# A one-core decoder step: splitting gate and output weights in the query phase and keeping the parts off chip

## Chip, core and metric

The kernel runs on one core of a Trainium2 chip. The metric is the time of one execution in microseconds of device time; the median of several runs is compared. TensorE (PE) multiplies matrices, VectorE (DVE), ScalarE (ACT) and GpSimd (POOL) work on tiles in SBUF, SyncE (SP) issues transfers. ACT and POOL issue transfers too.

## The reference, cut to what matters

```python
def rmsnorm(x, g):
    y = x * rsqrt(mean(x * x, -1) + 1e-6); return y * g
# xp: 1024 prompt tokens, xs: 8 new tokens; w_in is 1024 x 2840, w_out 1024 x 1024
q, ckv, skv, wkv, gl, za, u, zp = split(rmsnorm(x, norm_g) @ w_in, ...)
kv_c = silu-MLP over overlapping 32-token blocks of ckv       # compressed keys and values
o_attn = sum over 3 branches of sigmoid(gl) * softmax-attention(q, branch's K, V)
o_pool = ((trailing mean of u over 2/4/8/16) - u) @ w_pool * pool_scale
mix = concat([o_attn * silu(za), o_pool * silu(zp)])
y = rmsnorm(x + mix @ w_out, final_g)
```

The same is done for the 8 new tokens against a paged cache of 256 positions ("decode"). Everything is float32.

## The kernel before

A float32 product is made of three faster ones: each operand is split into a high part (a copy to float32r) and a low part (the rest), and high x high, high x low and low x high are summed in PSUM. Splitting weights is a copy on ACT and a subtraction, mostly on DVE (`split_w`, L142; `load_tile`, L387).

The program goes through these phases, which overlap:

1. Keys and values of all tokens (L303 to L376).
2. The query phase. The compression of the compressed branch (L460 to L525) and the four query tiles (L528 to L542) stand next to each other and are mixed by a scheduler, which orders the instructions of each engine when the program is built, by the priority that follows from the program text and by when it reckons each one ready. A query tile is `load_tile` for 128 columns of w_in and three `feat_unit`s (L400) of 24 matmuls, for token chunks of 384, 384 and 264 columns. The results of a unit go to one of two PSUM banks in turn (`ps_any`, L71); ACT and DVE empty it, and the query parts go off chip to q_d through ACT's queue. The compression runs twice ("kind" 0 and 1: keys and values): for three groups, POOL's queue brings four `pr` tiles (L437 from the new keys, L440 gathered from the cache), PE transposes them (`z_ps`, L475), ACT and DVE split them into zh and zl, and PE multiplies them with cmp_w1 (`h_ps`, L489 to L491). H (L497) is the activation, then follow kc_ps (kind 0) or vc_ps and vcs_ps (kind 1), and POOL stores Kcs and Vcs to kc_d.
3. The pooling phase (L801 to L859): per group a tile u (three feat_units, copied by ACT at L808) and a tile sz (three more), and in between, with high priority, the decode (L548).
4. The attention (L1159 to L1196): 32 units of `stage1` (scores S, softmax) and `stage2` (transposes tp, products into O). Between their matmuls `paced_fill` puts filler work: `za_fill` (L970) with the gate path's weights, loaded by `load_tile` and multiplied like a feat_unit; then, per token tile, the output product with the output weights, which `load_wo` (L990) loads and splits into the space of the chunk of x that za_fill has finished with. `load_q` (L727) brings the query parts back four units ahead.

`cp` and `qp` are the pools of the query phase, on the left side of SBUF; `pu` and `pp` those of the pooling phase, on the right side. Tiles that lie on the same bytes wait for each other.

Of the kernel before, what the change touches and what calls it, by code (L numbers as in the profile page):

```python
# [7 lines left out]
F32 = mybir.dt.float32  # L8
# [28 lines left out]
def r32(ap):  # L37
    return ap.bitcast(F32)
# [3 lines left out]
def hybrid_step_kernel(ctx, tc, xp, xs, ccmp, cslc, cwin, spool, ptab, norm_g, w_in, cmp_pe, cmp_w1,  # L42
# [36 lines left out]
    b_d = dram.tile([4, 128, TOK], F32, name="b_d")  # L79
    g_d = dram.tile([NB, 24], F32, name="g_d")  # L80
    kc_d = dram.tile([2, 128, 128], F32, name="kc_d")


    ident = pers.tile([128, 128], F32, name="ident")
# [57 lines left out]
    def split_w(hi, lo, raw, eng=None):  # L142
        nc.scalar.activation(hi, raw, AF.Copy)
        (eng or nc.vector).tensor_sub(lo, raw, r32(hi))
# [252 lines left out]
    def w_cols(c0):  # L397
        return w_in.rearrange("(k p) c -> p k c", p=128)[:, :, c0:c0 + 128]
# [126 lines left out]
            nc.gpsimd.dma_start(kc_d[1], Vcs)  # L525


    for pt in range(4):  # L528
        hi, lo = load_tile(w_cols(C_Q + pt * 128))
        for c in range(3):  # L530
            p, t0, n = feat_unit(hi, lo, c)
            m = min(n, T - t0)
            qt_ = qp.tile([128, 2, 384], F32R, name="qhl")
            qh, ql = qt_[:, 0], qt_[:, 1]

            nc.scalar.activation(qh[:, :m], p[:, :m], AF.Copy, scale=-0.125)
            nc.vector.scalar_tensor_tensor(ql[:, :m], p[:, :m], -0.125, r32(qh[:, :m]),
                                           op0=OP.mult, op1=OP.subtract)
            if n > m:
                nc.vector.tensor_scalar(qs_t[:, pt, :], p[:, m:n], 0.125, None, op0=OP.mult)  # L540
            nc.scalar.dma_start(q_d[:, pt * 128:(pt + 1) * 128, t0:t0 + m].rearrange("f p t -> p f t"),
                                r32(qt_[:, :, :m]))  # L542
# [427 lines left out]
    def za_fill():  # L970
        w = {}
        for pt, c in ZORD:
            if pt not in w:
                w[pt] = load_tile(w_cols(C_ZA + pt * 128))
            hi, lo = w[pt]
            for t0, n in CHUNKS[c:c + 1]:
                p = ps_j()
                for k in range(8):
                    nc.tensor.matmul(p[:, :n], hi[:, k, :], xh[c][:, k, :], start=k == 0, stop=False)  # L979
                    nc.tensor.matmul(p[:, :n], hi[:, k, :], xl[c][:, k, :], start=False, stop=False)  # L980
                    nc.tensor.matmul(p[:, :n], lo[:, k, :], xh[c][:, k, :], start=False, stop=k == 7)  # L981
                    if k == 7:
                        gate(pt, t0, n, p)
                    yield
            if pt == 3:
                with tc.high_priority(2000):
                    load_wo(c)
        xt_es.close()

    def load_wo(c):  # L990

        rows = WROWS[c]
        w = xtp.tile([128, 2, CHUNKS[c][1] * 8], F32R, name=f"wo{c}", tag=f"x{c}")
        w = w[:, :, :512 * len(rows)].rearrange("p f (k c) -> p f k c", c=512)
        for j in range(0, len(rows), 2):
            half, k = rows[j]
            raw = rp.tile([128, 2, 512], F32, name="wo_raw", tag="r")
            nc.sync.dma_start(raw, w_out[k * 128:(k + 2) * 128, half * 512:half * 512 + 512]
                              .rearrange("(k p) c -> p k c", p=128))
            for kk in range(2):  # L1000
                nc.scalar.activation(w[:, 0, j + kk], raw[:, kk], AF.Copy)
                (nc.vector, nc.gpsimd)[kk].tensor_sub(w[:, 1, j + kk], raw[:, kk], r32(w[:, 0, j + kk]))
                O_[half, k + kk] = w[:, 0, j + kk], w[:, 1, j + kk]

    def open_out():
        fp, op = (ctx.enter_context(tc.tile_pool(name=n, bufs=1, side="right", reuse_waits="tile"))
# [275 lines left out]
```

## Time and profile before

| | us |
|---|---|
| median of 3 runs (lowest, highest) | 639.88 (638.89, 640.13) |
| the profiled execution's own time | 638.69 |
| its span, first to last instruction | 637.0 |
| PE busy | 622.3 |
| DVE busy | 423.4 |
| ACT busy | 367.3 |
| POOL busy | 270.7 |

The difference between time and span, 1.7 us, lies around the instructions. Busy time of PE says that a matmul was under way, not that the engine worked at its peak. The rows below name engine, line, operation, the tile written and the tiles read; an arrow and a name behind a wait tell what ended it.

### The profile page before, as it was taken

How to read it: one execution, taken by the hardware profiler on the slowest of the kernel's cores; microseconds unless marked ns; L12 is line 12 of the kernel's file. 1: busy time of each engine (PE TensorE's matmuls, PEld its weight loads, DVE VectorE, ACT ScalarE, POOL GpSimd, SP SyncE). 2: the span in 40 equal slices, each digit the busy share in tenths (PEclk: the TensorE clock that was granted, in tenths of full speed). 3: DMA queues.
4: the chain of work that ended last, by engine and by line, in shares of the span. 5: the costliest groups of instructions: out<-in, count | busy, mean ns of one | idle time of the engine just before them, and what ended most of it. 6: DMA issues, size and time to landing. Idle time of an engine off the chain costs nothing.

```text
span 637.0 us, 12211 instructions
## 1 busy us (share of the span) xinstructions
PE 622.3 (98%) x4160; PEld 578.5 (91%) x4160; DVE 423.4 (66%) x1253; ACT 367.3 (58%) x947; POOL 270.7 (43%) x412
## 2 busy tenths in 40 slices
PE   8999999999999999999999999999999999999995
PEld 5999999999999899999899899789999988898895
DVE  6754234637364647466887999778978787877653
ACT  5654233526223333217887988777877777776652
POOL 6144004314035615005556767645554556444510
PEclk9999999999999999999999999999999999999999
DMA  8436106956224433333313357313113030101101
GB/s 281 152 90 157 34 1 201 314 196 181 74 79 133 138 102 95 92 110 101 100 35 99 100 182 214 107 30 101 37 50 100 18 100 16 67 19 67 51 2 66
DMA packets 63742, 65.13 MB, mean 102 GB/s; under 512 B 4488, under 2 KB 55120, under 8 KB 63640
## 3 DMA queue, kind: packets, MB, share of 16 engines
q1 hardware_dynamic: 53631, 44.55, 23.4%
q0 software_dynamic: 4000, 12.76, 6.2%
q10 hardware_dynamic: 6048, 7.05, 3.2%
q8 instruction: 33, 0.54, 0.4%
q14 instruction: 30, 0.24, 0.1%
HBM read 50.98 MB, written 15.68 MB: 105 GB/s over the span
## 4 chain that ended last, share of the span: by engine, by line
PE 93%; DVE 2%; ACT 1%; issue 1%; DMA 1%; POOL 1%; DVEq 0%; POOLq 0%; ACTq 0%
PE pj L1053 14%; PE S L777 10%; PE tp L902 9%; PE pa L404 7%; PE pa L406 7%; PE pa L405 7%; PE O L920 5%; PE O L919 5%; PE pa L277 4%; PE pa L275 3%; PE pa L276 3%; PE pj L979 2%; PE pj L980 2%; PE pj L981 2%; PE xtp_ps L230 1%; PE pj L1057 1%
## 5 line engine op out<-in xcount | busy, mean ns | idle before, releaser
L908 DVE TENSOR_TENSOR pl<-tp,ph 128x512 fp32r<-128x512 f32 (+1 forms) x136 | 89.9, 670 | 22.7 <-ACT ph L907 22.0
L777 PE MATMUL S<-KT,qt 128*128 128x320 f32 (+10 forms) x400 | 98.2, 346 | 3.0 <-DVE sm L736 3.0
L907 ACT ACTIVATE ph<-tp 128x512 fp32r<-128x512 f32 (+1 forms) x136 | 78.0, 580 | 38.3 <-PE tp L902 28.7
L404 PE MATMUL pa<-x,ws_hi 128*128 128x384 f32 (+1 forms) x288 | 93.7, 325 | 0.0
L406 PE MATMUL pa<-x,ws_lo 128*128 128x384 f32 (+1 forms) x288 | 92.9, 323 | 0.0
L405 PE MATMUL pa<-x,ws_hi 128*128 128x384 f32 (+1 forms) x288 | 92.7, 322 | 0.0
L1053 PE MATMUL pj<-wo,mh 128*128 128x512 f32 (+1 forms) x272 | 84.1, 387 | 0.0
L920 PE MATMUL O<-pl,V 128*128 128x256 f32 x264 | 75.7, 305 | 0.2
L919 PE MATMUL O<-ph,V 128*128 128x256 f32 x264 | 74.0, 296 | 0.0
L777 PEld LDWEIGHTS S<-KT,qt 128*128 128x128 f32 x400 | 63.7, 189 | 9.0 <-DVE sm L736 3.0
L796 POOL TENSOR_SCALAR Ps<-Ps,sm,gates 128x64 f32<-128x64 f32 (+5 forms) x88 | 62.9, 722 | 19.9 <-DVE sm L792 7.3
L789 ACT ACTIVATE Ps<-Ps,sm 128x64 f32<-128x64 f32 (+4 forms) x96 | 60.2, 628 | 16.4 <-DVE sm L736 14.8
L404 PEld LDWEIGHTS pa<-x,ws_hi 128*128 128x128 f32 x288 | 54.2, 188 | 0.5
L405 PEld LDWEIGHTS pa<-x,ws_hi 128*128 128x128 f32 x288 | 54.2, 188 | 0.4 <-issue 0.3
L406 PEld LDWEIGHTS pa<-x,ws_lo 128*128 128x128 f32 x288 | 54.2, 188 | 0.2
L277 PE MATMUL pa<-w_hi,x 128*128 128x256 f32 (+1 forms) x184 | 52.9, 288 | 1.2 <-DVE x L236 1.2
L275 PE MATMUL pa<-w_hi,x 128*128 128x256 f32 (+1 forms) x184 | 53.6, 292 | 0.0
L1053 PEld LDWEIGHTS pj<-wo,mh 128*128 128x128 f32 x272 | 47.2, 188 | 6.1 <-ACT mh L1205 0.3
L920 PEld LDWEIGHTS O<-pl,V 128*128 128x128 f32 x264 | 49.8, 189 | 3.1 <-DVE pl L908 0.6
L276 PE MATMUL pa<-w_lo,x 128*128 128x256 f32 (+1 forms) x184 | 52.4, 285 | 0.0
L1053 PE MATMUL pj<-wo,ml 128*128 128x512 f32 (+1 forms) x136 | 52.1, 383 | 0.0
L919 PEld LDWEIGHTS O<-ph,V 128*128 128x128 f32 x264 | 49.9, 189 | 1.8
(302 smaller groups left out, 1556.1 us busy)
## 6 DMA issues: line engine op xcount, KB each, us to landing
ws_raw<-in_w_in SPq DMA_DIRECT2D x32, 256.0 KB, 3.1
qt<-q_d SPq DMA_DIRECT2D x64, 128.0 KB, 2.9
x_t<-in_x_prompt SPq DMA_DIRECT2D x8, 512.0 KB
wo_raw<-in_w_out SPq DMA_DIRECT2D x8, 512.0 KB, 4.3
r<-in_x_prompt SPq DMA_DIRECT2D x8, 512.0 KB, 3.1
out<-r SPq DMA_DIRECT2D x7, 512.0 KB, 3.1
q_d<-qhl ACTq DMA_DIRECT2D x8, 384.0 KB, 4.0
out<-kvf ACTq DMA_DIRECT2D x5, 512.0 KB, 3.1
```

The source lines that it names most:

```text
L275: nc.tensor.matmul(p[:n, :cn], xh[c][:, k, ts_], hi[:, k, :cn], start=k == 0, stop=False)
L276: nc.tensor.matmul(p[:n, :cn], xh[c][:, k, ts_], lo[:, k, :cn], start=False, stop=False)
L277: nc.tensor.matmul(p[:n, :cn], xl[c][:, k, ts_], hi[:, k, :cn], start=False, stop=k == 7)
L404: nc.tensor.matmul(p[:, :n], hi[:, k, :], xh[c][:, k, :], start=k == 0, stop=False)
L405: nc.tensor.matmul(p[:, :n], hi[:, k, :], xl[c][:, k, :], start=False, stop=False)
L406: nc.tensor.matmul(p[:, :n], lo[:, k, :], xh[c][:, k, :], start=False, stop=k == 7)
L777: nc.tensor.matmul(S[:, :ln], qt[:, f, h, :], KT[:, kv, k0 + a:k0 + a + ln], start=f == 0, stop=f == 1)
L907: nc.scalar.activation(ph[:, :m], tp[:, :m], AF.Copy)
L908: nc.vector.tensor_sub(pl[:, :m], tp[:, :m], r32(ph[:, :m]))
L919: nc.tensor.matmul(O[:, :256], vv, ph[:, a * 256:(a + 1) * 256], start=False, stop=False)
L920: nc.tensor.matmul(O[:, :256], vv, pl[:, a * 256:(a + 1) * 256], start=False, stop=last)
L1053: nc.tensor.matmul(p, a[:, k % 4, :], w, start=first and kk == 0, stop=last and kk == 2)
```

## The change

While the query phase runs, 24 pieces are staged: 8 halves of the four za weight tiles and 16 pieces of w_out, six ahead of each query tile. A piece is loaded by POOL's queue into `sraw` (2 buffers), split by ACT and DVE into `sw` (high and low part side by side, 2 buffers) and stored by POOL's queue to zw_d or wo_d. Later `load_za` and `load_wo` fetch both parts through SP's queue, straight into the tiles that the matmuls read. Nothing is split in the attention any more.

```diff
+    wo_d = dram.tile([2, 8, 128, 2, 512], F32, name="wo_d")
+    zw_d = dram.tile([4, 2, 128, 2, 512], F32, name="zw_d")
...
+    to_stage = [(zw_d[pt, h], w_cols(C_ZA + pt * 128)[:, 4 * h:4 * h + 4], 4) for pt in range(4) for h in range(2)]
+    to_stage += [(wo_d[half, k], w_out[k * 128:(k + 1) * 128, half * 512:half * 512 + 512], 1)
+                 for rows in WROWS for half, k in rows]
+
+    def stage_some(n):
+        for dst, src, k in to_stage[:n]:
+            raw = cp.tile([128, 512], F32, name="sraw", bufs=2)
+            nc.gpsimd.dma_start(raw.rearrange("p (k c) -> p k c", k=k) if k > 1 else raw, src)
+            w = cp.tile([128, 2, 512], F32R, name="sw", bufs=2)
+            split_w(w[:, 0], w[:, 1], raw)
+            nc.gpsimd.dma_start(dst, r32(w))
+        del to_stage[:n]
+
+    def load_za(pt):
+        hi = ws.tile([128, 8, 128], F32R, name="ws_hi", bufs=2)
+        lo = ws.tile([128, 8, 128], F32R, name="ws_lo", bufs=2)
+        for h in range(2):
+            for f, w in enumerate((hi, lo)):
+                nc.sync.dma_start(r32(w[:, 4 * h:4 * h + 4].rearrange("p k c -> p (k c)")), zw_d[pt, h, :, f])
+        return hi, lo
+
     for pt in range(4):
+        stage_some(6)
         hi, lo = load_tile(w_cols(C_Q + pt * 128))
...
-                w[pt] = load_tile(w_cols(C_ZA + pt * 128))
+                w[pt] = load_za(pt)
...
-        for j in range(0, len(rows), 2):
-            half, k = rows[j]
-            raw = rp.tile([128, 2, 512], F32, name="wo_raw", tag="r")
-            nc.sync.dma_start(raw, w_out[k * 128:(k + 2) * 128, half * 512:half * 512 + 512]
-                              .rearrange("(k p) c -> p k c", p=128))
-            for kk in range(2):
-                nc.scalar.activation(w[:, 0, j + kk], raw[:, kk], AF.Copy)
-                (nc.vector, nc.gpsimd)[kk].tensor_sub(w[:, 1, j + kk], raw[:, kk], r32(w[:, 0, j + kk]))
-                O_[half, k + kk] = w[:, 0, j + kk], w[:, 1, j + kk]
+        for j, (half, k) in enumerate(rows):
+            nc.sync.dma_start(r32(w[:, :, j]), wo_d[half, k])
+            O_[half, k] = w[:, 0, j], w[:, 1, j]
```

The new tiles take 12 KB per partition of `cp`, so `qp` lies 12 KB higher. Addresses in the built programs, in bytes of a partition: before, cp and qp end at 126752 and the two u tiles of the pooling phase lie at 130304 to 134496 and 134496 to 138688. With the change sraw lies at 120608 to 124704, the second sw buffer at 128800 to 132896, and the two qhl buffers of the query parts at 132896 to 139040.

The scheduler orders all engines anew. In the new file, lines of the query phase and after have numbers that are up to 26 higher. Names behind "waits" are semaphores: PE, DVE and Activation count those engines' instructions, DMASW0 to DMASW7 count landings of POOL's transfers in turn, DMAHW those of SP's and ACT's.

ACT at the end of the compression, before: the first u copies (L808) stand ahead of H of kind 1 (L497).

```order
L541 DMA q_d<-qhl 128x2x256 [waits DVE_49]
L808 ACTIVATE u<-pa 128x384 [waits PE_49]
L480 ACTIVATE zh<-z_ps 64x8x64 [waits PE_49] x2
L480 ACTIVATE zh<-z_ps 64x8x64 [waits DVE_49] x2
L808 ACTIVATE u<-pa 128x384 [waits PE_49]
L497 ACTIVATE H<-h_ps,hb 128x384 [waits DVE_49,PE_49]
L143 ACTIVATE ws_hi<-ws_raw 128x512 [waits DMAHW7_49,PE_49]
```

The same place with the change (L499 is H, L519 Vc, L834 the u copy, L145 the copy of split_w):

```order
L145 ACTIVATE sw<-sraw 128x512 [waits DMASW5_49,DMASW4_49,DVE_49]
L499 ACTIVATE H<-h_ps,hb 128x384 [waits DVE_49,PE_49]
L145 ACTIVATE sw<-sraw 128x512 [waits DMASW7_49,DMASW6_49,Activation_49]
L519 ACTIVATE Vc<-vc_ps 64x2x64 [waits PE_49]
L519 ACTIVATE Vc<-vc_ps 64x2x64 [waits DVE_49]
...
L145 ACTIVATE sw<-sraw 128x512 [waits DMASW2_49,DMASW1_49,DVE_49]
L145 ACTIVATE sw<-sraw 128x512 [waits DMASW4_49,DMASW3_49,DVE_49]
L834 ACTIVATE u<-pa 128x384 [waits DMAHW6_49,DMASW6_49,DVE_49]
L834 ACTIVATE u<-pa 128x384
L145 ACTIVATE ws_hi<-ws_raw 128x512 [waits DMAHW7_49,PE_49]
```

Seventeen of the 24 sw copies stand ahead of H and all of them ahead of the first u copy; the landing that DMASW6 counts there is that of the last store to wo_d.

POOL from the four gathers of kind 1 on, with the change (L442 is the gather, L538 a staging load, L541 a staging store, L526 and L527 the stores of Kcs and Vcs):

```order
L442 DMA pr<-in_cache_cmp_kv,idx 128x512 [waits PE_49]
L541 DMA wo_d<-sw 128x1024 [waits DMASW5_49,DVE_49]
L538 DMA sraw<-in_w_out 128x512 [waits DMASW6_49]
L526 DMA kc_d<-Kcs 128x128 [waits DMASW7_49,DVE_49]
L541 DMA wo_d<-sw 128x1024 [waits DMASW0_49,DVE_49]
L538 DMA sraw<-in_w_out 128x512 [waits DMASW1_49]
L442 DMA pr<-in_cache_cmp_kv,idx 128x512 [waits DMASW2_49,PE_49]
L442 DMA pr<-in_cache_cmp_kv,idx 128x512 [waits DMASW3_49,PE_49]
L541 DMA wo_d<-sw 128x1024 [waits DMASW4_49,DVE_49]
L538 DMA sraw<-in_w_out 128x512 [waits DMASW6_49,DMASW5_49]
```

Before, the two stores of kc_d and the gathers were all that stood there. The first staging store in this piece is that of item 8 (items counted from 0), and the pattern of a store and a load goes on to item 23, with the store of Vcs behind the load of item 19. The last six stores stand behind that of Vcs, ahead of the decode's first instructions on POOL.

PE at the end of kind 1, before:

```order
L406 MATMUL pa<-x_90,ws_lo 128x384
L513 MATMUL vc_ps<-w2v,H 64x64 x2
L521 MATMUL vcs_ps<-w2v,H 128x64 x2
L810 MATMUL ut<-ident,u 15x128
```

and with the change (L515 and L523 are vc_ps and vcs_ps, L493 the last line of h_ps, L406 to L408 feat_unit):

```order
L493 MATMUL h_ps<-zl,ws_hi 128x386
L515 MATMUL vc_ps<-w2v,H 64x64 x2
L523 MATMUL vcs_ps<-w2v,H 128x64 x2
L406 MATMUL pa<-x_94,ws_hi 128x264
L407 MATMUL pa<-x_94,ws_hi 128x264
```

Before, 384 matmuls of feat_unit stand ahead of vc_ps: 288 of the queries, 72 of the first u and 24 of the first sz. With the change it is 336: the queries' and two chunks of the first u; its third chunk comes right behind vcs_ps. Ahead of kc_ps (kind 0), and so ahead of kind 1's transposes, it was 240 and is 272.

## Rows read from the trace of the kernel before

**Rows 1.** The page: span, and section 1 (busy us, share, instructions of each engine)

```profile
span 637.0 us, 12211 instructions
PE 622.3 (98%) x4160; PEld 578.5 (91%) x4160; DVE 423.4 (66%) x1253; ACT 367.3 (58%) x947; POOL 270.7 (43%) x412
```

**Rows 2.** Windows: stretch, us, busy by engine (instructions), granted clock, DMA share, GB/s

```profile
98.00:190.00 92.00, 92.00 (x590) 90.64 (x588) 48.53 (x116) 35.80 (x71) 26.17 (x34) 1.00 0.59 181
...
285.00:420.00 135.00, 131.37 (x903) 121.42 (x902) 109.52 (x419) 107.89 (x337) 85.09 (x143) 1.00 0.37 112
420.00:560.00 140.00, 140.00 (x908) 126.78 (x907) 115.55 (x364) 104.09 (x255) 70.61 (x100) 1.00 0.19 58
```

**Rows 3.** Waits from 285 us on: who waited for whom, us, times, longest

```profile
PE S L777 <- DVE sm L736: 3.0, 6, 1.0
```

**Rows 4.** Instructions of load_tile and load_wo: ns min/median/max, first and last start

```profile
L143 ACT ACTIVATE ws_hi<-ws_raw x40: 613/630/634, 50.9 to 326.8; 128x512 fp32r<-128x512 f32 x40
...
L144 DVE TENSOR_TENSOR ws_lo<-ws_raw,ws_hi x40: 678/692/1672, 51.6 to 328.8; 128x512 fp32r<-128x512 f32 x40
...
L1001 ACT ACTIVATE wo<-wo_raw x16: 615/628/637, 354.6 to 398.3; 128x512 fp32r<-128x512 f32 x16
...
L1002 POOL TENSOR_TENSOR wo<-wo_raw,wo x8: 1283/1324/1719, 358.3 to 399.0; 128x512 fp32r<-128x512 f32 x8
```

**Rows 5.** Issues on POOL: pr tiles (128 pieces) and psc (512 pieces of 4 bytes)

```profile
L437 POOL DMA_DIRECT2D pr<-out x8: 536/548/627, 101.9 to 126.9; - x8
...
L378 POOL DMA_DIRECT2D psc<-in_pool_scale x1: 845/845/845, 47.3 to 47.3; - x1
```

**Rows 6.** Transfers from 98 to 190 us: queue and count, KB each, median us to landing

```profile
ws_raw<-in_w_in SPq DMA_DIRECT2D x10, 256.0 KB, 7.3
ws_raw<-in_cmp_w SPq DMA_DIRECT2D x8, 256.0 KB, 3.1
pr<-out POOLq DMA_DIRECT2D x8, 256.0 KB, 4.6
```

**Rows 7.** The page, section 6: a large store from POOL's queue

```profile
b_d<-bb POOLq DMA_DIRECT2D x4, 516.0 KB, 3.0
```

**Rows 8.** Windows as in rows 2: the query phase's transfers

```profile
98.00:160.00 62.00, 62.00 (x400) 61.01 (x398) 35.00 (x83) 28.46 (x56) 22.16 (x28) 1.00 0.75 232
110.00:120.00 10.00, 10.00 (x64) 9.68 (x64) 5.43 (x10) 5.44 (x10) 2.83 (x3) 1.00 1.08 347
```

**Rows 9.** Timeline of ACT: start us, us, instruction, idle before it and what ended it

```profile
162.30 0.49 ACT L808 ACTIVATE u<-pa 128x384 f32<-128x384 f32 x1 [1.59 <-PE pa L406]
...
177.50 0.58 ACT L497 ACTIVATE H<-h_ps,hb 128x384 f32<-128x384 f32 x1 [9.88 <-DVE hb L495]
...
183.09 0.26 ACT L517 ACTIVATE Vc<-vc_ps 64x128 fp32r<-64x128 f32 x1
```

**Rows 10.** Timeline of POOL: the first and the fourth gather of kind 1 that wait

```profile
149.83 0.94 POOL L440 DMA_INDIRECT pr<-in_cache_cmp_kv,idx  x1 [19.76 <-PE z_ps L475]
...
153.58 0.95 POOL L440 DMA_INDIRECT pr<-in_cache_cmp_kv,idx  x1 [0.30 <-issue]
```

**Rows 11.** Timeline of PE: the same matmul of two units, 24 apart; two of 264 columns

```profile
98.91 0.33 PE L405 MATMUL pa<-x,ws_hi 128*128 128x384 f32 x1
...
103.07 0.33 PE L405 MATMUL pa<-x,ws_hi 128*128 128x384 f32 x1
...
107.06 0.28 PE L404 MATMUL pa<-x,ws_hi 128*128 128x264 f32 x1
107.18 0.28 PE L405 MATMUL pa<-x,ws_hi 128*128 128x264 f32 x1
```

**Rows 12.** Windows as in rows 2: the first and the last 5 us

```profile
0.00:5.00 5.00, 3.74 (x8) 1.75 (x9) 1.18 (x4) 1.70 (x2) 3.31 (x14) 1.00 0.55 173
...
632.00:637.00 5.00, 0.00 (x0) 0.00 (x0) 0.90 (x3) 0.67 (x1) 0.00 (x0) 0.72 0.27 105
```

## The prediction, made before the changed kernel had run

> **What bounds the kernel now.** I read the page first: TensorE is busy for 622.3 of 637.0 us [rows 1]. Then the windows by stage, to see where the missing 15 us lie: none in the query phase, 98 to 190 us, where PE is busy for 92.00 of 92.00 us; 3.6 us in the early attention, 285 to 420 us; none from 420 to 560 us [rows 2]. The list of waits says what the early attention's idle time is: six waits of S for VectorE's row minimum, 3.0 us [rows 3]. The rest stands at both ends of the program. So whatever ScalarE, VectorE or GpSimd are spared in the attention can bring 3.6 us at most, and any wait of PE that is new in the query phase costs its whole length, because no idle time behind it can take it up. The question is whether the staging stays out of PE's way.
>
> **What is removed.** In the attention the za tiles lose 8 splits and load_wo loses 16 half splits: 24 ACT copies of 0.63 us (15.1 us), 16 subtractions on DVE and 8 on POOL of 1.3 us [rows 4]. PE waits for none of these lines; it could win from a freer DVE in the six waits of [rows 3]. Bounds: 0 and 3.6 us of gain. I take 1 us, since those waits are for L736 itself, whose own work is unchanged. The loads that take their place bring 256 KB pieces straight into the weight tiles. They wait on SP for a tile that PE has read to its end, with the qt loads queued behind them; a qt is asked for four units ahead, and 32 units share the 345 us after 285 us, 10.8 us each, so this is hidden by some 40 us and costs nothing. Were the lead gone, each such wait would cost the 3 to 4 us of one landing.
>
> **What is added, and fits.** 24 items, each: a 256 KB load and a 512 KB store issued by POOL, a copy on ACT, a subtraction on DVE. ACT gets 24 x 0.63 = 15 us and DVE 24 x 0.69 = 17 us in a stretch where they are busy for 36 and 49 of 92 us [rows 2, 4]: by sums it fits. POOL gets 48 issues at about 0.57 us [rows 5], 27 us beside 26 us of 92. The eight za loads are cut into 512-byte pieces, 512 to a load, which the trace has no issue of; its nearest are 0.55 us with 128 pieces and 0.85 us with 512 tiny ones [rows 5], so 0.55 to 0.85 each, at most 2.4 us in all, while POOL waits for PE anyway: nothing.
>
> **What is added, and is on the path.** Two facts of the order and of the addresses, shown with the change, decide. The first u tile of the pooling phase now lies partly on the second sw buffer, and ACT's first u copy stands behind all 24 sw copies and waits for the last staging store to land. Before, it waited for PE alone and ran at 162.3 us, in the middle of the compression [rows 9]. PE needs that copy: u chunks 0 and 1 fill both banks of ps_any, and chunk 2, next on PE after vcs_ps, needs the first one back. So PE stops there until the last store lands. When is that?
>
> The store chain hangs on POOL's order. Items 0 to 9 go in pieces between the pair gathers, which wait for PE's z_ps transposes as before. The four gathers ahead of store 8 began at 149.83 us [rows 10]; PE's new order puts 32 more feat matmuls ahead of their transposes. A matmul of 384 columns takes 4.16 / 24 = 0.173 us, one of 264 takes 0.12 [rows 11], the mean over the chunks is 0.155, so 32 x 0.155 = 5.0 us: the fourth gather begins at 153.58 + 5.0 = 158.6 and ends at 159.5 us. Store 8 is issued then, and load 10 at 160.1 us.
>
> From there to the end POOL holds little but store, load, store, load, and each load waits for the store ahead of it, which waits for the split of the load two items before. One turn serves two items (two buffers): issue of a store 0.57, the load's landing, copy 0.63, subtraction 0.69, three handovers of 0.07 (an estimate: the first ws copy starts at 50.9 and takes 0.63, its subtraction starts at 51.6 [rows 4]). The landing is the disputed size: 3.1 us for 256 KB where the queues are quiet, 4.6 for the pair tiles on this same queue, 7.3 for the worst kind in this phase [rows 6]. I take 4.6, same queue and size. A turn is 0.57 + 4.6 + 1.52 = 6.7 us. Store 10: 160.1 + 4.6 + 1.52 = 166.2. Six turns later store 22: 206.4. Store 23 follows at 207.5 and lands after 3.0 us, the time of a 516 KB store from POOL [rows 7]: 210.5. The u copy takes 0.5: **PE goes on at 211.0 us**. With 3.1 it is 200.5, with 7.3 it is 229.9.
>
> What that costs: at ACT's first Vc copy, 183.1 us [rows 9], PE had 384 feat matmuls behind it; in the new order it has 336 when it stops. The missing 48 (24 of 264 columns, 24 of 384) are 7.0 us. Loss: 211.0 + 7.0 - 183.1 = **34.9 us**; bounds 24.4 and 53.8.
>
> Part of this stop falls earlier, and is not to be added: H of the second kind stands on ACT behind sw 16, so PE waits there first (sw 16 comes three turns after sw 10, at about 185 us, where H ran at 177.5).
>
> The bytes must fit too. The 24 items move 24 x 768 KB = 18.9 MB. At the highest rate that a 10 us window shows, 347 GB/s at a share of 1.08 [rows 8], that is 54 us. The work already there takes 0.75 x 62 = 46.5 us from 98 to 160 us [rows 8]. Together 101 us: not before 199 us without a gap. So the chain of landings (211 us) binds, and the quiet 3.1 us landing is already near what the bytes allow. [...]
>
> Two smaller prices. Items 0 to 7 run at 108 to 148 us, where the engines are fullest: the gathers may land later and PE's transposes wait. Nearest rows: the waits of PE in this phase are nil with landings of 7.3 us about, so 0; above, one late landing of 7.3 instead of 4.6 at each of two groups, 5 us. [...] I take 0 for both and keep 12 us above.
>
> **Sum.** 638.69 us is the profiled execution's own time (span 637.0). 638.69 - 1 + 34.9 = 672.6; the median of the runs shown is 1.2 us above that execution, so I say **673 us**.
>
> **Rivals.**
> 1. *Quick landings (slower, but less).* Nothing else is on the queue after 165 us, and landings fall to 3.1: loss 24.4 and the full gain of 3.6, 638.69 + 24.4 - 3.6 = 659.5 us. For it: by 160 us the phase's own gathers and most of its weights are in; against it: two 512 KB stores now go beside every two loads. [...]
> 2. *Clogged engines.* Landings of 7.3 us: loss 53.8, 691 us, and up to 703 us with the two smaller prices.
> 3. *Faster.* The staging ends before PE has run out of work, at 183.1 - 7.0 = 176 us, which is the point from which it decides. Then only the gain is left: 635 us at best. It needs 14 items in the 16 us after store 8, 1.1 us each, against 2.6 us by the quickest landing.
> 4. *The wait isn't there* (the tiles don't meet in practice): within 0.2%. The built program's wait excludes it almost wholly.
>
> **Chances.** My forecast, 666 to 686 us: 0.70. Rival 1, 653 to 666: 0.14. Rival 2, above 686: 0.11. Rival 3: 0.03. Rival 4: 0.02. About 0.2% (1.3 us) is what a measurement of this kernel can tell from no change. Faster 0.03, same 0.02, slower 0.95. The range goes from 658, just under rival 1's 659.5, to 694 us, just over rival 2's 691; it leaves out the faster cases, the lowest part of rival 1 and the part of rival 2 with the smaller prices on top.
>
> **What would show it.** Right: PE idle for about 35 us in all between 165 and 215 us, in one or two blocks whose releasers are ACT's H and u copies; the u copy's own releaser a DMA to wo_d; POOL's stores and loads spaced by about 6.7 us a turn after 166 us; PE as dense as before from 215 us on; the attention's S waits still some 2 us. Wrong: the last wo_d store landing before 195 us, or PE idle mostly elsewhere (z_ps transposes waiting for pr, or attention matmuls waiting for ws_hi or wo); then the place or the size of my term falls.

## The result, and the profile after

**684.5 us** (median of 4 runs, 683.3 to 687.2) against 640.0 (4 runs, 638.9 to 640.2): the ratio is 1.070, 95% interval 1.067 to 1.074, slower by 44.5 us. The forecast was 673 in a range of 658 to 694, with 0.95 on slower. The profiled execution took 685.2 us.

The page of the changed kernel, span, busy time, PE and its clock by slices:

```profile
span 683.5 us, 12346 instructions
PE 627.0 (92%) x4160; PEld 584.4 (86%) x4160; DVE 428.6 (63%) x1261; ACT 369.6 (54%) x947; POOL 282.7 (41%) x452
PE   8999999989521999999999999969999999999996
PEclk9999999999865999999999999999999999999999
```

Against [rows 1] the span is 46.5 us longer; PE does the same 4160 matmuls and is busy for 4.7 us more. So some 42 us are idle time; the 4.7 us go with a slower clock, 0.968 granted in the mean of the profiled run instead of 0.998. The slices (17 us each) show where: a hole in slices 11 to 13, around 200 us, and dents in 9 and 27.

Windows (columns as in [rows 2]), first two of the kernel before, then those of the changed one:

```profile
0.00:240.00 240.00, 235.55 (x1619) 224.77 (x1620) 121.63 (x271) 98.62 (x222) 79.87 (x120) 1.00 0.47 143
220.00:240.00 20.00, 20.00 (x128) 18.71 (x129) 10.18 (x28) 8.46 (x22) 5.67 (x9) 1.00 0.40 118
```

```profile
0.00:240.00 240.00, 197.55 (x1331) 186.36 (x1331) 117.94 (x241) 98.86 (x212) 93.25 (x147) 0.92 0.61 200
98.00:160.00 62.00, 58.20 (x367) 56.45 (x366) 33.41 (x76) 27.65 (x53) 28.59 (x39) 1.00 0.90 298
160.00:180.00 20.00, 12.70 (x78) 11.46 (x77) 14.29 (x27) 11.39 (x22) 10.51 (x15) 0.90 0.94 336
180.00:200.00 20.00, 11.73 (x56) 10.79 (x56) 6.49 (x14) 4.79 (x9) 8.10 (x15) 0.76 0.72 249
200.00:220.00 20.00, 0.00 (x0) 0.00 (x0) 3.90 (x10) 3.52 (x6) 7.11 (x12) 0.50 0.71 239
220.00:240.00 20.00, 19.84 (x113) 18.48 (x113) 12.54 (x33) 6.56 (x17) 8.99 (x16) 0.90 0.28 80
330.00:465.00 135.00, 127.65 (x902) 122.97 (x902) 100.84 (x406) 100.39 (x312) 69.92 (x130) 0.99 0.51 155
```

By 240 us PE has done 1331 matmuls instead of 1619. The kernel before does 128 in 20.00 us, 0.156 us each, so it is 288 x 0.156 = 45.0 us behind: nearly the whole loss has happened by then. This count, **the delay at 240 us**, is used for every run below; it is an estimate, since some matmul records may be missing and matmuls of different sizes are counted alike.

PE's waits in the changed kernel (who waited for whom, us, times, longest):

```profile
PE pa L406 <- ACT u L834: 25.1, 1, 25.1
PE S L803 <- DMA qt<-q_d: 4.4, 2, 3.6
PE h_ps L491 <- ACT zh L482: 4.0, 2, 3.2
PE vc_ps L515 <- DVE H L501: 3.4, 1, 3.4
PE z_ps L477 <- DMA pr<-in_cache_cmp_kv,idx: 2.9, 2, 2.7
PE pj L1073 <- ACT mh L1053: 2.4, 1, 2.4
```

Before, the longest was the row minimum's [rows 3]; that wait is gone from the list. The 25.1 us are the forecast's stop. ACT's and POOL's timelines (start, us, instruction, idle before it and what ended it) show both ends of it:

```profile
169.34 2.65 ACT L482 ACTIVATE zh<-z_ps 64x512 fp32r<-64x512 f32 x4 [4.14 <-PE z_ps L477]
172.02 0.63 ACT L145 ACTIVATE sw<-sraw 128x512 fp32r<-128x512 f32 x1
...
219.62 0.87 ACT L834 ACTIVATE u<-pa 128x384 f32<-128x384 f32 x2 [3.99 <-DMA wo_d<-sw]
```

```profile
164.40 0.59 POOL L541 DMA_DIRECT2D wo_d<-sw  x1
...
173.84 0.58 POOL L541 DMA_DIRECT2D wo_d<-sw  x1 [1.86 <-DVE sw L146]
...
212.07 0.54 POOL L541 DMA_DIRECT2D wo_d<-sw  x1 [0.83 <-DVE sw L146]
216.65 0.54 POOL L541 DMA_DIRECT2D wo_d<-sw  x1 [4.04 <-DVE qs L580]
```

Store 8 goes at 164.4 (forecast 159.5), store 10 at 173.8 (166.2), store 22 at 212.1 (206.4), store 23 at 216.65 (207.5), and the first u copy starts at 219.6 (210.5). It waited for the last store, as foretold.

### The profile page after: what moved, and what is told of

It is laid out like the page before. It is cut to its first block, busy times and chain, and to the rows that moved or that the text cites. A ratio compares the mean times of both kernels' runs of the same rounds, so it can differ in the third digit from the quotient of the medians.

```text
span 683.5 us, 12346 instructions
## 1 busy us (share of the span) xinstructions
PE 627.0 (92%) x4160; PEld 584.4 (86%) x4160; DVE 428.6 (63%) x1261; ACT 369.6 (54%) x947; POOL 282.7 (41%) x452
## 4 chain that ended last, share of the span: by engine, by line
PE 77%; DMA 13%; issue 4%; DVE 2%; POOL 2%; ACT 2%; SPq 0%; DVEq 0%; POOLq 0%; ACTq 0%
PE pj L1073 13%; PE S L803 8%; PE tp L928 7%; PE pa L406 5%; PE pa L407 5%; PE pa L408 5%; PE O L946 4%; PE O L945 4%; PE pa L279 3%; PE pa L277 3%; PE pa L278 3%; DMA qt<-q_d 3%; DMA ws_raw<-in_w_in 2%; DMA sraw<-in_w_out 2%; PE pj L1006 2%
## 5 line engine op out<-in xcount | busy, mean ns | idle before, releaser
L406 PE MATMUL pa<-x,ws_hi 128*128 128x384 f32 (+1 forms) x288 | 94.9, 330 | 27.8 <-ACT u L834 25.1
L408 PE MATMUL pa<-x,ws_lo 128*128 128x384 f32 (+1 forms) x288 | 93.3, 324 | 0.0
L406 PEld LDWEIGHTS pa<-x,ws_hi 128*128 128x128 f32 x288 | 55.0, 191 | 29.0 <-ACT u L834 25.3
L803 PEld LDWEIGHTS S<-KT,qt 128*128 128x128 f32 x400 | 65.1, 191 | 8.5 <-issue 4.3
L407 PEld LDWEIGHTS pa<-x,ws_hi 128*128 128x128 f32 x288 | 55.0, 191 | 0.3
L408 PEld LDWEIGHTS pa<-x,ws_lo 128*128 128x128 f32 x288 | 54.9, 191 | 0.2
```

The source lines that it names most:

```text
L803: nc.tensor.matmul(S[:, :ln], qt[:, f, h, :], KT[:, kv, k0 + a:k0 + a + ln], start=f == 0, stop=f == 1)
```

## The experiments

All differences are taken to the kernel before, run beside each on the same chip. "Delay" is the delay at 240 us, "span" the profiled span less 637.0. The profiled execution is one of a run's several: it lies 3.7 us below the median in e4 and 1.7 us above it in e8, so spans of two runs are compared to no better than that.

| run | median us | ratio (95%) | matmuls by 240 us | delay | span |
|---|---|---|---|---|---|
| changed | 684.5 | 1.070 (1.067-1.074) | 1331 | 45.0 | +46.5 |
| e1_u_other_buffer | 684.4 | 1.072 (1.070-1.073) | 1337 | 44.1 | +45.3 |
| e2_gate_only | 661.3 | 1.035 (1.034-1.037) | 1524 | 14.8 | +22.7 |
| e4_staged_unused | 686.7 | 1.075 (1.074-1.077) | 1351 | 41.9 | +44.3 |
| e5_fetch_only | 654.0 | 1.026 (1.023-1.029) | 1548 | 11.1 | +14.7 |
| e6_three_raw | 690.9 | 1.083 (1.081-1.084) | 1339 | 43.8 | +51.8 |
| e8_u_second_buffer | 685.1 | 1.072 (1.071-1.074) | 1336 | 44.2 | +48.1 |
| e12_gpsimd_splits_last | 690.2 | 1.080 (1.078-1.082) | 1310 | 48.3 | +50.6 |
| e9_pad_only | 643.3 | 1.008 (1.005-1.010) | 1591 | 4.4 | +3.9 |
| e5q_query_tile_kept | 652.5 | 1.021 (1.020-1.022) | 1598 | 3.3 | +14.6 |
| e7_mb_ahead | 652.8 | 1.022 (1.020-1.025) | 1548 | 11.1 | +14.0 |
| e13_high_part_fetched | 651.2 | 1.019 (1.017-1.021) | 1548 | 11.1 | +11.8 |
| e14_gate_staged_earlier | 642.0 | 1.005 (1.003-1.007) | 1602 | 2.7 | +3.0 |

**The two halves, and the gate path alone.** e4 puts the old loads back and stages for nothing; e5 keeps the new fetches and stages one piece of each kind; e2 stages and fetches the gate path only. In e4 and e2 load_wo is that of the kernel before; in e5 load_za reads zw_d[0, 0].

```diff
# e4
-                w[pt] = load_za(pt)
+                w[pt] = load_tile(w_cols(C_ZA + pt * 128))
# e5
-    to_stage = [(zw_d[pt, h], w_cols(C_ZA + pt * 128)[:, 4 * h:4 * h + 4], 4) for pt in range(4) for h in range(2)]
+    to_stage = [(zw_d[pt, h], w_cols(C_ZA + pt * 128)[:, 4 * h:4 * h + 4], 4) for pt in range(1) for h in range(1)]
...
-                 for rows in WROWS for half, k in rows]
+                 for rows in WROWS[:1] for half, k in rows[:1]]
...
-            nc.sync.dma_start(r32(w[:, :, j]), wo_d[half, k])
+            nc.sync.dma_start(r32(w[:, :, j]), wo_d[WROWS[0][0]])
# e2
-    to_stage += [(wo_d[half, k], w_out[k * 128:(k + 1) * 128, half * 512:half * 512 + 512], 1)
-                 for rows in WROWS for half, k in rows]
...
-        stage_some(6)
+        stage_some(2)
```

> Everything is staged as in the changed kernel, but what was stored is never fetched: gate path and output weights are loaded and split in the attention as before. Theory (the loss is in the query phase; the fetches on SP's in-order queue cost another 4 us in the attention, where TensorE's waits went from 3.6 to 7.4 us): 678 to 682. Rival (the ready-made fetches gain a little, as the removed splits took ScalarE and VectorE time): over 684, up to 688. Second rival (the fetches carry much of the loss): below 670.

> The other half by itself: all later fetches are made as in the changed kernel (same queue, same sizes, ready-made high and low parts), but only the first piece of the gate path and the first of the output weights are split and stored, and every fetch reads that one. So the weights of the gate path and of the output product are left out but for one piece of each. Theory (the fetches on SP stand in front of the query tiles and cost more than the removed splits give): TensorE's waits between 330 and 465 us stay near 7 us instead of 3.6, and the time is 641 to 646 against 640. Rival (my forecast's reading: splitting was on the path for up to 3.6 us and the fetches are hidden): 636 to 639. A third case, nothing either way: 639.5 to 640.5.

> Only the gate path's 8 pieces are staged (two in each of the four query groups); the output weights are loaded and split in the attention as in the kernel before, one third of the staging stores is left. Theory (a chain of 24 load-copy-subtract-store turns of 6.4 us over two buffers, whose last store ends after u is due): 8 items are through before the gathers of the key phase end, at some 160 us, 45 us before u is due; the stop of 25 us is gone, what is left is the early waits of 3 to 10 us: 642 to 652. Rival (transfer contention and the splitting work slow the query phase in proportion to what is staged): a third of the loss of 44 us goes with a third of the staging, 655 to 665. A second rival (the gate part costs most, since its pieces are 512 short runs): over 670.

Staging without any fetch costs all of it: 686.7 (683.0 to 687.3) against the changed kernel's 684.5 (683.3 to 687.2), two sets that lie over each other. So nearly all of the loss is made by staging. The time is in the range of the first rival (684 to 688), but the gain from the fetches on which that rival rests is too small to tell here. But e5, with hardly any staging, still loses 15 us, more than any case had it, and the two halves add up to 59 us of span for the whole's 46.5: something is in both. e2 lies in the proportional rival's range, though none of its PE waits is for staging: its last store is issued at 155.7 us, before PE needs u. Most of e5's loss, 11.1 us, is there by 240 us. Two of PE's five waits for the compression (the other three are for pr tiles, 0.6 to 0.9 us each):

```profile
173.04 0.69 PE L491 MATMUL h_ps<-zh,ws_hi 128*128 128x386 f32 x1 [2.63 <-ACT zh L482]
186.72 0.42 PE L515 MATMUL vc_ps<-w2v,H 128*64 128x64 f32 x4 [2.13 <-DVE H L501]
```

These are the compression's own short waits. In the kernel before, feat matmuls stood on PE between z_ps, h_ps and vc_ps and covered them; here none stand between the last z_ps and vc_ps.

**Is that the addresses?** Staging's 12 KB move the query tile under u, so the scheduler issues no feat matmul there, with or without traffic. e9 is the kernel before with those 12 KB and nothing else; e5q is e5 with the query tile back at its old address, and sraw and sw in a pool sp behind it.

```diff
# e9
     NCOL = 384
+    for name, n in (("sraw", 512), ("sw", 1024)):
+        for _ in range(2):
+            nc.gpsimd.memset(cp.tile([128, n], F32, name=name, bufs=2)[:, :1], 0.0)
# e5q
     qp = ces.enter_context(tc.tile_pool(name="qp", bufs=2, reuse_waits="tile"))
+    sp = ces.enter_context(tc.tile_pool(name="sp", bufs=2, reuse_waits="tile"))
```

> The kernel before with nothing of the change but its addresses: staging's two load tiles and two split tiles (12 KB) are allocated at the foot of the compression's pool and one column of each is written, so that the query tile goes up by 12 KB and lies under the first pooling group's u, as in the changed kernel. No staging, no fetch, no transfer more. The order in which PE's instructions are issued then has no pooling matmul between the second kind's h_ps and vc_ps, where the kernel before has 34, 3 and 35. Theory (the smaller part of the loss is this: short waits of the compression that lie bare, each with a low granted clock behind it): waits of PE for zh, H and the query tile of 4 to 7 us, as in the fetch-only kernel, and 644 to 650. Rival (the order does not matter, the traffic did it): 638 to 641.

> The fetch-only kernel (one piece of gate path and output weights each, all later fetches of these) took 654 us, 15 more than the kernel before, though it stages 2 pieces only; TensorE stood still for 7 us in the query phase and worked at a lower granted clock behind that. Here its staging tiles come after the query tile instead of ahead of it, so that the query tile keeps the address it had in the kernel before (120608 to 126752) and u lies on the staging tiles only, which are done early. As in that run, all but one piece each of the gate and output weights are left out. Theory (staging's 12 KB push the query tile under u, so the u copy waits for the query tiles' stores and pooling matmuls no longer cover the compression's short waits): the query phase is whole again and the attention's 5 us remain: 643 to 648. Rival (it is the two staged pieces' traffic on the queues): 652 to 656.

e9 is slower by 4.1 us (3.4 to 6.1), all of it by 240 us, with no transfer and no split more: the addresses and the order that follows from them have a price of their own. It lies just under the 644 to 650 that I expected and above the rival's 641, and PE's waits are shorter than the 4 to 7 us that I expected. PE's one long wait from 98 to 240 us in e9:

```profile
PE vc_ps L516 <- DVE H L502: 2.0, 1, 2.0
```

In e5q the query phase is whole again, as the theory had it, and yet the time is the rival's. The loss has moved. Windows of e5q:

```profile
98.00:200.00 102.00, 101.58 (x650) 100.17 (x648) 50.02 (x120) 39.12 (x78) 25.66 (x33) 1.00 0.57 178
285.00:330.00 45.00, 40.58 (x261) 37.90 (x260) 23.76 (x131) 25.20 (x104) 16.77 (x40) 0.92 0.39 112
```

From 285 to 330 us it does 261 matmuls where the kernel before did 304, PE is idle for 4.4 us instead of 1.4, and the granted clock is 0.92 instead of 1.00. That the new addresses bared this place while they cured the other is argued, not shown. So e5's 11 us are the addresses' 4 and others that I did not take apart.

**What the stop hangs on.** In e1 a spare tile was to push u to its second buffer; nothing wrote it, so it was left out of the program, and e1 is a second measurement of the changed kernel. e8 writes one column of it; e12 also has GpSimd split the last six items, so that ACT's u copy stands behind item 17.

```diff
# e1
+    pu.tile([128, H0 + TOK], F32, name="u", bufs=2)
     for g in range(4):
# e8
+    nc.vector.memset(pu.tile([128, H0 + TOK], F32, name="u", bufs=2)[:, :1], 0.0)
     for g in range(4):
# e12, against e8
-            split_w(w[:, 0], w[:, 1], raw)
+            if len(to_stage) > 6:
+                split_w(w[:, 0], w[:, 1], raw)
+            else:
+                nc.gpsimd.tensor_copy(w[:, 0], raw)
+                nc.gpsimd.tensor_sub(w[:, 1], raw, r32(w[:, 0]))
```

(len(to_stage) counts this group's items too, so in e12 the last group's six are meant.)

> The changed kernel with one line more: the pool of u hands out its second buffer first, so that the first pooling group's u lies where only a long finished tile lay, and the second group's u, not the first, lies on staging's split tile. Nothing of the staging itself is changed: same transfers, same order, same copies. Theory (PE stops because the first u copy waits for the last staging store to read its tile out): the stop moves behind one pooling group, whose three features (72 matmuls at about 0.2 us, some 15 us at full clock) TensorE runs inside the time in which it now stands still; 684 becomes 667 to 671, and the idle time in front of the group-0 copy (25.1 us) falls to 8 to 12 us in front of the group-1 copy. Rival (the transfers of staging slow the whole phase, and the wait on the tile is where it shows, not why): the bytes are the same, 682 to 686.

> The first run of this study was to give the first pooling group the second u buffer, but its spare tile was never written and so was dropped; here one column of it is written, and u of group 0 lies at 134496 to 138688, on the query tiles alone and clear of staging's. Theory (PE's 25 us stop is the wait of that copy for the last staging store): the copy now waits only for the query tiles' stores, PE goes on with group 0 after the compression, and meets staging's tile a group later: 666 to 672, the longest wait of PE below 12 us. Rival (the staging traffic itself holds the phase up, whatever tile it lies on): 681 to 686.

> The kernel with u of group 0 on the second buffer (685 us; there ACT's first u copy at 216.3 us stood directly behind its copy for staging item 23, and waited no longer for a store), with one thing more: the last six items are split on GpSimd instead of ScalarE and VectorE, so that the u copy stands behind item 17 on ScalarE. Transfers and their order are the same. Theory (ScalarE's program order is a sufficient cause of the stop by itself, the address another): the u copy runs at 195 to 202 us, the longest wait of PE is below 8 us, 684 becomes 664 to 674; GpSimd's own split, slower, may give a few us back where the decode part waits for its gathers. Rival (the traffic of staging holds the phase up): 681 to 688.

e8 missed: 685.1. ACT's timeline in e8:

```profile
215.73 0.63 ACT L145 ACTIVATE sw<-sraw 128x512 fp32r<-128x512 f32 x1 [3.96 <-DMA sraw<-in_w_out]
216.27 0.85 ACT L835 ACTIVATE u<-pa 128x384 f32<-128x384 f32 x2
```

u's tile is free and its operand has been ready since PE stopped, but the copy stands behind the last sw copy, which waits for its load: ACT's program order alone holds PE for 21.5 us, and the address adds only the last store's landing (219.6 instead of 216.3). Little of that reaches the time: e8's delay is 44.2 us, the changed kernel's 45.0.

e12 missed too, and shows the same on another engine. The u copy ran when it should (ACT), then PE met the next wait (PE's list), for VectorE, which stood before its own write of a u tile until the last store had landed (DVE):

```profile
194.90 0.87 ACT L839 ACTIVATE u<-pa 128x384 f32<-128x384 f32 x2
```

```profile
PE dsc L639 <- DVE qs L597: 26.1, 1, 26.1
PE pa L406 <- ACT u L839: 2.5, 1, 2.5
```

```profile
225.46 0.06 DVE L831 MEMSET u<- 128x1 f32 x1 [30.08 <-DMA wo_d<-sw]
```

That write is the spare tile's, which e8 and e12 brought in themselves: it lies on staging's split tile. So in all three the stop comes where the engine whose result PE needs stands at an instruction that waits for staging's end: ACT for 3.99 us (the changed kernel) and 3.96 us (e8), DVE for 30.08 us (e12). That PE would run on through all 24 items with no engine so held was not tried.

**What sets the chain's pace.** e6 gives staging a third load tile.

```diff
# e6
-            raw = cp.tile([128, 512], F32, name="sraw", bufs=2)
+            raw = cp.tile([128, 512], F32, name="sraw", bufs=3)
```

> The changed kernel with three staging load tiles in place of two, so that a third load can be under way while two items are copied, subtracted and stored. Bytes and work are the same. Theory (the chain is bound by the latency of its turns: a load lands, is split, its tile comes free, the next load is issued): two items a turn of 6.4 us become three, the 14 items after the gathers take some 30 us instead of 45, the last store lands at 200 to 206 us instead of 221, and 684 becomes 664 to 674. Rival (the 16 engines are full, so more loads in flight only land later): 681 to 686.

Missed: 690.9. ACT's waits, first of the changed kernel, then of e6:

```profile
ACT sw L145 <- DMA sraw<-in_w_out: 29.4, 13, 4.0
```

```profile
ACT sw L145 <- DMA wo_d<-sw: 25.3, 12, 3.7
```

The wait for the loads went, and nearly as long a one for the stores came: there are two loops over two buffers, load to split to next load, and split to store to next split. Stores 10 and 22 in e6:

```profile
174.99 0.58 POOL L541 DMA_DIRECT2D wo_d<-sw  x1 [2.75 <-DVE sw L146]
...
210.29 0.54 POOL L541 DMA_DIRECT2D wo_d<-sw  x1 [2.59 <-DVE sw L146]
```

That is 5.9 us for two items, where the changed kernel takes 6.4 and I had expected 4.3. So the chain did go faster, until the store's loop held it, and its last store went out 2.0 us sooner (214.6). The time gained nothing: from 98 to 160 us PE was idle for 8.0 us instead of 3.8, and e6 lost 8 us more behind 240 us, where one wait of S for a query tile was 6.8 us long. Why these grew was not taken apart.

The transfers from 175 to 215 us in e8 (queue and count, KB each, median us to landing), which has the changed kernel's buffers:

```profile
wo_d<-sw POOLq DMA_DIRECT2D x12, 512.0 KB, 3.8
sraw<-in_w_out POOLq DMA_DIRECT2D x11, 256.0 KB, 4.2
```

From 180 to 220 us, with a share of 0.71 to 0.72 and 239 to 249 GB/s in the windows above, under the 347 of [rows 8], the engines were not full (from 160 to 180 us, at 0.94 and 336, they nearly were); in e6 they moved 291 GB/s at a share of 0.81 from 180 to 200 us, where the changed kernel moved 249. This speaks for latency over two buffers; a third buffer for both, which would prove it, was not run.

**The fetches in the attention.** From 330 to 465 us PE is idle for 7.35 us in the changed kernel, against 3.63 in the same stretch of the work before, 285 to 420 us [rows 2] (902 matmuls and 903). SP's timeline shows the fetches of wo, which are issued only when PE gives a tile back (three waits of SP for PE, 44.2 us in all), and what stands behind them:

```profile
422.02 4.30 SPq L1022 DMA_DIRECT2D wo<-wo_d  x6
426.37 0.81 SPq L1213 DMA_DIRECT2D out<-in_cache_win_kv  x1
...
427.97 4.89 SPq L758 DMA_DIRECT2D qt<-q_d  x4
440.21 7.35 SPq L1022 DMA_DIRECT2D wo<-wo_d  x4
...
449.17 0.38 SPq L1042 DMA_DIRECT2D mb<-b_d  x1
```

The qt tiles land behind 3 MB of fetches and a copy of 2 MB, and PE's S waits (4.4 us); mb, the first output tile's load, waits for the third set. Two runs take e5 (where PE waited 4.8 us for mh, the split of mb): e7 puts mb ahead of the third set (load_wo(2) is called in filler(), behind the first out_half's loads), e13 fetches the high part only.

```diff
# e7
-            if pt == 3:
+            if pt == 3 and c < 2:
                 with tc.high_priority(2000):
                     load_wo(c)
# e13
-            nc.sync.dma_start(r32(w[:, :, j]), wo_d[WROWS[0][0]])
-            O_[half, k] = w[:, 0, j], w[:, 1, j]
+            nc.sync.dma_start(r32(w[:, 0, j]), wo_d[WROWS[0][0]][:, 0])
+            O_[half, k] = w[:, 0, j], w[:, 0, j]
```

> The fetch-only kernel again (same weights left out), but the third set of output-weight fetches stands behind the first output tile's own loads on SP instead of ahead of them. Theory (the new fetches wait on SP for TensorE to give a tile back, and the loads queued behind them come late; PE's wait of 4.8 us for the first output tile and the low granted clock in the 25 us behind it are that): 645 to 650 against 654. Rival (the fetches' traffic, 8 MB instead of 4, is what makes these loads land late): 652 to 656.

> The fetch-only kernel (654 us), where of the output weights only the high part is fetched, 256 KB a piece instead of 512, and stands for the low part too; the same matmuls run on it. So the low part of the output weights is left out, beside what the fetch-only kernel leaves out. Waits for TensorE to give back a tile, number of fetches, their order on SP are the same. Theory (PE's wait of 4.8 to 6.7 us for the first output tile comes from bytes: 3 MB of fetches, bunched because they wait for the tile, and the first output tile's 256 KB load takes 8 to 11 us to land beside them): the load lands in 4 to 6 us, PE's wait is below 2 us, 654 becomes 644 to 650. Rival (it is SP standing still until the tile is free): 651 to 655.

e7 missed: its interval overlaps e5's, and PE's wait for mh grew to 6.7 us. SP in e7:

```profile
391.06 10.04 SPq L1029 DMA_DIRECT2D fg<-in_final_g  x1
...
403.15 0.38 SPq L1042 DMA_DIRECT2D mb<-b_d  x1
404.37 3.15 SPq L1022 DMA_DIRECT2D wo<-wo_d  x4
```

The order is as wanted, but the issue of fg took 10.0 us, with the engines at a share of 1.00 and more from 385 to 395 us, so mb went out 3.7 us sooner than in e5 (406.9) and then had the third set beside it, with the engines at a share of 1.05 from 405 to 410 us. e13, with half the bytes, is the first that helps: 12.1 us over the kernel before instead of 15.3, intervals apart, PE's wait 3.4 instead of 4.8, and 0.7 us lost behind 240 us instead of 3.6 (span less delay). It lies at the lower edge of the rival's 651 to 655 and above the theory's 650: the bytes are part of it, the wait for the tile leaves the other part, and I cannot divide them further.

**The same pieces at another place.** e14 stages and fetches the gate path's eight pieces as e2 does, but in the key and value phase, one behind each token tile, in tiles of their own (pool sg) that close before the query phase; to_stage and stage_some stand ahead of that loop.

```diff
# e14, against e2
+    sg = sgs.enter_context(tc.tile_pool(name="sg", bufs=2, side="right", reuse_waits="tile"))
     for br in range(2):
...
             p, n = tok_unit(hi, lo, cn, t)
+            if br == 0 and t < 8:
+                stage_some(1)
...
+    sgs.close()
     tmaj.close()
...
     for pt in range(4):
-        stage_some(2)
```

> The same eight gate pieces staged and fetched as in the run with the gate path alone (661 us), but staged during the key and value phase (30 to 98 us, where the 16 engines are busy for a quarter of the time), one behind each of the first eight token tiles, on tiles of their own that end before the query phase begins. Output weights as in the kernel before. PE's instruction order is that of the kernel before. Theory (what the change costs is its place: ScalarE's order, the address under u, the traffic beside the gathers; ready-made gate weights themselves cost nothing and can give back at most some of the 3 us of waits in the early attention): 637 to 642. Rival (a staged and fetched piece costs some 2.8 us wherever it is done, 22 us for eight): 655 to 662. If it is below 637.5 it beats both kernels.

642.0 us, 2.9 over its kernel before (2.0 to 4.2) where e2 is 22.6 over: the same splits, stores and fetches, and 20 us of difference. The place is the cost, with the addresses and the order that come with it. It is at the upper edge of the theory and beats nothing. Between 285 and 330 us it does win what the forecast allowed for, PE 44.98 us busy instead of 43.60, and loses it again: 1.6 us less work from 30 to 98 us, and one bare wait for ACT with a clock of 0.96 from 375 to 420 us:

```profile
PE O L947 <- ACT ph L935: 2.2, 1, 2.2
```

## Why the prediction held, and where it was off

**Right.** The direction; the place; the releaser; the chain's pace. Turns from store 10 to store 22 took (212.07 - 173.84) / 6 = 6.37 us for the 6.7 of "A turn is 0.57 + 4.6 + 1.52"; the last store landed in 3.0 us as said. Rival 3's deciding point, staging's end at 176 us, was missed by over 40 us. PE is idle for 35.6 us from 160 to 220 us, where the forecast's sign was about 35. That is partly luck: the sign named one or two blocks and there are six waits, 25.1 us ending with the u copy, 3.4 with H (by VectorE's part of it, not ACT's), the rest with zh, pr and zl. The floor by bytes of 199 us did not bind.

**"PE goes on at 211.0 us"** was 9 us early: it was 220. Four steps make that up. "Items 0 to 7 ... so 0": the gathers ended 4.9 us late, mostly since PE idled for 3.8 of the 62 us from 98 to 160. It waited there not for pr tiles, as the forecast feared, but for copies: 1.4 and 1.3 us for those that empty the banks of the queries, 1.1 us for the compression's splits. Before one of them ACT stood until an earlier store of the queries had landed, with the engines at a share of 1.07 from 120 to 130 us (0.85 before):

```profile
128.16 0.38 ACT L562 ACTIVATE qhl<-pa 128x256 fp32r<-128x256 f32 x1 [2.57 <-DMA q_d<-qhl]
```

So this is the forecast's own "Two smaller prices", whose first it took at 0 and bounded by 5 us; it came at the bound. Of the late landings behind it only this one is shown.

"Store 10: 160.1 + 4.6 + 1.52": it came 9.4 us after store 8, not 6.7, because its copy stood on ACT behind four zh copies (172.02 above), 2.7 us. The six turns gave back 2.0. Store 23 followed store 22 by 4.6 us, not 1.1: an item's load is issued only behind the store ahead of it, so one buffer's items come late and the other's early, 3.5 us. 4.9 + 2.7 - 2.0 + 3.5 = 9.1.

**"I take 0 for both and keep 12 us above"** was wrong for the clock too. No run shows the 7 of these 12 us that were kept for a slower clock behind the stop; what the runs showed is less. The granted clock is 0.50 while PE stands ([rows 12] have 0.72 in the last 5 us, with PE idle) and 0.90 from 220 to 240 us, where PE does 113 matmuls in place of 128: 15 x 0.156 = 2.3 us. By size it is somewhat less: the first 16 behind the stop, of 264 columns, take 3.7 us, 0.23 each where [rows 11] have 0.12, so 1.8 us.

**The attention: "this is hidden by some 40 us and costs nothing"** was wrong in its mechanism. The lead of four units was used up on SP: a fetch waits for PE to return a tile, and the qt and mb loads behind it on the same queue go out late and land late; mb, issued at 449.2 us, was there for its split at 459.8. From 240 us on the changed kernel lost about 1.5 us more (46.5 - 45.0) where I had it gain 1.

**Two facts decide, said the forecast, the address and ACT's order.** ACT's order is enough alone (e8), and so is the address where DVE meets it (e12); in the changed kernel the address adds some 3 us to what ACT's order costs. What it did not see at all is the third: the moved query tile alone costs 4 us (e9), by uncovering short waits of the compression. In the changed kernel these lie in front of the stop, so it hid most of them: with the stop, PE would have waited anyhow. That would be why the halves do not add; it is argued, not shown.

9.1 us of stop, 1.8 to 2.3 of clock and 2.5 of attention make 13.4 to 13.9 us, where 12.6 lie between the sum (672.6) and the profiled execution (685.2); the difference is within what the count of matmuls can tell. The forecast's last step has a slip: 672.6 and 1.2 make 673.8, not 673.

**Open:** what e5 loses by 240 us beyond the addresses' 4 us; how bytes and the wait for the tile share the attention's part.

## What to carry to other kernels

Work that is spread over idle engine time still stands in each engine's program order: here ACT's first u copy stood behind copies that waited for landings, and PE for 21.5 us behind it (e8), so count the landings ahead of the first instruction that the bound engine needs, not the busy shares. When a change adds tiles, look at which tiles then lie on which, and at what that does to the order, before the costs of the added work: here 12 KB without any work cost 4 us. A chain over two buffers has two loops, the load's and the store's, and widening one alone gains only until the other holds it (5.9 us a turn instead of 6.4 here, and nothing in the time).

## What the runs showed of the hardware

**Waits of PE cost more than their length here.** Windows of e7 around the wait of 6.7 us for mh, and PE's matmuls of one size in the second and the last:

```profile
405.00:410.00 5.00, 0.00 (x0) 0.00 (x0) 1.72 (x7) 0.00 (x0) 0.00 (x0) 0.74 1.05 319
410.00:415.00 5.00, 3.44 (x13) 3.24 (x14) 1.23 (x3) 3.52 (x9) 3.41 (x5) 0.50 1.12 303
415.00:420.00 5.00, 5.00 (x20) 4.14 (x19) 1.12 (x5) 1.06 (x4) 2.48 (x4) 0.74 0.90 206
420.00:425.00 5.00, 5.00 (x35) 4.66 (x34) 3.44 (x13) 3.26 (x9) 0.46 (x1) 1.00 0.15 48
```

```profile
412.80 0.41 PE L945 MATMUL O<-ph,V 128*128 128x256 f32 x1
...
420.78 0.28 PE L945 MATMUL O<-ph,V 128*128 128x256 f32 x1
```

PE stands from 405 to 410, and the granted clock falls to 0.50 while it works again (410 to 415 us). From 411.6 to 417.7 us it takes 6.2 us for eight matmuls of 512 columns, ten of 256 and two of 320. Behind that, with the clock back up (1.00 from 420 us on), starts of the same sizes are 0.23, 0.12 and 0.16 us apart, at which the twenty would take 3.3 us. So the clock adds 2.9 us to the wait of 6.7. Shorter waits too had a low clock behind them: in e9 the two idle times at 177 and 179 us, 2.0 and 0.6 us, are followed by these 5 us, at 0.53:

```profile
180.00:185.00 5.00, 5.00 (x25) 5.00 (x25) 1.78 (x9) 0.17 (x1) 1.66 (x3) 0.53 0.11 32
```

In e2 PE is busy for 631.1 us instead of 622.3 with the same matmuls: 8.8 of its 22.7 us are, by that, the slower clock (0.983 in the mean of the profiled run, against 0.998 before), though none of its waits was longer than 3.6 us.

**One issue on SP took 10.0 us behind transfers that were under way.** fg took 10.04 us to issue in e7, right behind some 5 MB; the engines' share was 1.00 and more up to 395 us and 0.47 from 395 to 400. In e5, where the same issue goes out behind the third set, at 405.4 us, it took 0.39. The four wo fetches of the third set took 7.35 us together in the changed kernel and 2.59 in e13, with half the bytes. What SP waits for inside such an issue no row shows.
